# The low-part score products of the banded attention over all 128 rows, with zeros beside the keys' low parts

## The chip, the cores and the metric

One core of one Trainium2 chip runs the whole program. The metric is the device time of one execution in microseconds (us); the kernel before was run three times. A profile of one execution was taken beside the timed runs, and every row below is from it.

## What is computed

Two layers of a bidirectional encoder over 256 tokens with 1024 features. In each layer three branches are mixed (latent attention, a Fourier transform, banded attention), and a SwiGLU and a gated embedding follow. The change touches the scores of the banded attention alone:

```
q = q.reshape(B, nb, WIN_BLOCK, GQA_KV_HEADS, GQA_GROUP, GQA_HEAD_DIM)   # 2 key heads x 4 query heads, 64 wide
...
s = jnp.einsum('bnqhgd,bnkhd->bnhgqk', q, kw).astype(jnp.float32) * scale
s = s - slopes[None, None, :, :, None, None] * dist[:, :, None, None]
...
s = jnp.where(mask[None, :, None, None], s, -jnp.inf)
m = jnp.maximum(jnp.max(s, axis=-1, keepdims=True), sink_l)
e = jnp.exp(s - m)
probs = (e / (jnp.sum(e, axis=-1, keepdims=True) + jnp.exp(sink_l - m))).astype(v.dtype)
o = jnp.einsum('bnhgqk,bnkhd->bnqhgd', probs, vw)
```

There are 8 query heads of 64 features; heads 0 to 3 share the first key head ("left"), heads 4 to 7 the second ("right").

## The kernel before

**Numbers in two parts.** TensorE multiplies in a format that keeps 12 significant bits. Every float32 operand a is therefore split on chip into a high part H (a copy on ScalarE, rounded) and a low part L = a - H (a subtraction on VectorE), and a product takes three passes: H H, H L and L H. The weights stream in as chunks of eight 128 x 128 tiles (`w`, split to `wh` and `wl` at lines 175 and 180); activations live in the tiles `mixH` and `mixL` (in the code `A22` and `B22`: 22 slots of 128 x 256 each), `xs_...` (the layer's input) and others.

**Order of work.** A small planner in the program (class `Order`) writes the order of TensorE, ScalarE and VectorE out ahead of time, with assumed durations: 0.109 us for each product of 256 columns, whatever its rows. The main line is the products on TensorE; side chains (softmax, splits, norms) are woven in when the plan says that their data are there. On the chip each engine runs its own list in that order, and semaphores hold an instruction until its inputs are written. GpSimd (POOL) is not ordered by the planner: it does a few memsets, the norms' inverse roots (`rt_...`, line 497) and small copies.

**The banded attention.** In each layer `window_k` writes the keys and `window_qsplit` the queries. A head is 64 features wide, so a head's high and low parts fit on the 128 rows together: `qcs` holds, for a left head, the queries' high parts on rows 0 to 63 and their low parts on rows 64 to 127 (for a right head the other way round), and `kcs` holds the keys' high parts on both halves. One product of `qcs` with `kcs` over 128 rows is thus H H + L H. The third pass, the queries' H with the keys' L, takes only the 64 rows where the queries' high parts lie; the keys' low parts are in slot `KCI` of `B22`, the left head's on rows 0 to 63, the right head's on rows 64 to 127. `window_head` (8 per layer, two in flight, started 5.6 us apart in the plan) issues for each of two blocks of 128 queries the full product (line 977) and the 64-row product (line 978) into one tile `sc`; then VectorE adds the distances (line 289, out `sbc`), takes the maximum (line 984), ScalarE the exponentials, TensorE the transposes (`ptc`, line 924), and after a split (`phc`, `plc`) the products with the values (`po`, line 948). Between these steps TensorE does the Fourier transform (`pu`, `pab`, lines 317 to 319), the gates (`gp`) and the branches (`br`), lines 357, 358 and 364. Line 503 turns an inverse root into rows (`pr_...`), and cannot start before POOL's `rt_...`.

The latent attention later in the layer has heads of 128 rows: its scores (`sa`, lines 317 to 319 too) are three full passes for each block of queries.

Of the kernel before, what the change touches and what calls it, by code (L numbers as in the profile page):

```python
# [9 lines left out]
F32 = mybir.dt.float32  # L10
# [20 lines left out]
# the order of work is laid out with these times in us  # L31
T_MM = 0.109                # a float32r product with 256 columns
T_SEM = 0.18                # from one engine to another
MIX = "CCGGCCPPGPPGGBGGGBGGGBBG" # what fills attention's waits: Fourier channels and positions, gates, branches
TAB = 18.0                  # when the rotary tables are made
PACE = 5.6                  # from one head's start to the next
LATER = 0.3                 # how long a chain waits before its next step
ONACT = 2                   # of how many heads one is normed on ScalarE
STAGE = 3                   # buffers for weights as they come
WARM = (0.33, 0.15)         # how long TensorE is kept busy without data  # L40
URGENT = (4.5, 2.5)         # how far behind ScalarE and VectorE may be for splits to go on
LATE = (2, 2, 2)            # operand tiles left to a product's end
CT = 8                      # weight tiles of 128 x 128 per load
NCHUNK = 279

# columns of the constants' array
# [16 lines left out]
def dft_tiles():  # L63
    """The DFT over a group's 256 channels (cosines of 0..127, the alternating column, sines of
    1..127) and over the 256 positions, each with half of the orthonormal scale."""
    n = np.arange(256)
    cos = np.cos(2 * np.pi * (np.outer(n, n) % 256) / 256) / 16.0
    sin = np.sin(2 * np.pi * (np.outer(n, n) % 256) / 256) / 16.0
    m2 = np.concatenate([cos[:, :128], sin[:, :128]], axis=1)
    m2[:, 128] = cos[:, 128]  # L70
    return np.stack([m.reshape(2, P, SEQ).transpose(1, 0, 2) for m in (m2, cos, sin)]).astype(np.float32)
# [6 lines left out]
class Order:  # L78
    """Lays out the order of every engine's work: a main line of products on TensorE, and side chains
    that hand data from engine to engine. A chain gives the time at which its next piece's inputs  # L80
    should be there, and the piece goes in when the main line has come that far."""
# [19 lines left out]
    def run(self, engine, us, *deps):  # L101
        """an instruction on another engine; gives the time at which its result can be used"""
        at = max(self.free[engine], self.now, *deps)
        self.free[engine] = at + us
        return at + us + T_SEM

# [18 lines left out]
    def wait(self, at):  # L125
        """the main line needs something that is there at this time"""
        assert at < 1e8
        while self.now < at:
            to = min([at] + [max(t[0], self.now) for t in self.tasks])
            if self.warm:  # L130
                self.warm(to - self.now)
            self.now = to
            self.step()


class Weights:
    """The weights as one stream of 128 x 128 tiles in the order of their use; each is split on chip
    into two parts of 12 significant bits, w = H + L, both exact in float32r."""
# [17 lines left out]
    def pieces(self, c):  # L156
        n = CT * P // (1 if c else 2)       # the first chunk comes in halves
        return [slice(k, k + n) for k in range(0, CT * P, n)]

    def split(self):  # L160
        """a chain: the next chunk's parts, and the load of one more chunk"""
# [22 lines left out]
    def idle(self, engine, c, us):  # L184
        """waits while the engine has other work, unless the chunk is needed within this time"""
        O = self.O
        while (self.quiet or O.free[engine] > O.now + 0.1) and (c * CT - len(self.order)) * 3 * T_MM > us:
            yield O.now + 0.3

    def flush(self, n=0):  # L190
        """starts the splits that are due and have their buffers"""
        self.due += n
        while self.due and not self.using.get(len(self.parts) - 3):
            self.due -= 1
            self.O.start(self.split())

    def ready(self, n=1, high=False):
        """the time at which the next n tiles can be used"""
        c, at = (len(self.order) + n - 1) // CT, self.at_h if high else self.at
        return at[c] if c < len(at) else 1e9  # L200
# [21 lines left out]
def encoder(ctx: ExitStack, tc: tile.TileContext, order, gxT, pT, pos, cst, dftT, mask, sink, wts, outT):  # L222
# [21 lines left out]
    rd = {}                 # what chains have made, and when it can be used  # L244

# [16 lines left out]
    def drop(t, at=0.0):  # L262
        """its last use is in the order, and ends at this time"""
# [4 lines left out]
    def line(gen):  # L268
        """a chain's piece on the main line"""
# [31 lines left out]
    def need(key):  # L301
        """in a chain: goes on when this is there"""
# [5 lines left out]
    def have(key):  # L308
        """on the main line"""
# [24 lines left out]
    def mains(ps, keys, rhs, start=True, stop=True, skip=False, there=None):  # L334
        """a column tile's products over tiles of the contraction; those with a chunk's low parts come last"""
        i = 0
        while i < len(keys):
# [9 lines left out]
            # what the waits let in may have taken tiles  # L347
# [23 lines left out]
    def k_outer(pairs, key, rhs, done, late):  # L371
        """pairs of column tiles, each pair in a bank of its own, over the contraction's 8 tiles; over its
        last ones pair by pair"""
# [28 lines left out]
    def keep_warm(step):  # L402
        """while the main line waits, products of zeros hold TensorE's clock up"""
# [38 lines left out]
    class Squares:  # L442
        """sums of squares over feature tiles: six in pairs, and the last two one by one"""
# [4 lines left out]
        def add(self, src):  # L448
            """a chain's piece; src: [P, 2, SEQ]"""
# [21 lines left out]
        def total(self):  # L471
            """the pairs' sum"""
# [3 lines left out]
        def total1(self):  # L476
            """and the first single tile"""
# [12 lines left out]
    def rms_cols(ps, norms, name):  # L490
        """1/rms per token, as columns"""
# [8 lines left out]
    def rms_rows(pr, rt, n):  # L500
        """the columns as rows on every partition"""
# [4 lines left out]
    def rstd(parts, name):  # L506
        """parts: (tiles whose sum over partitions and tiles is the sum of squares, D, eps), up to two"""
# [29 lines left out]
    def pre_norm(st, name):  # L537
        """a chain: x's squares and the next products' 1/rms"""
# [11 lines left out]
    def post_norm(st, y, sq, i, nxt, name, want_squares, final=False, gname=None):  # L550
        """A chain: x += y * rstd(y) (times a gain if that isn't in y); splits the new x (times the next norm's gain) for
        the next products. Starts when seven tiles of y are under way."""
# [116 lines left out]
    def tables():  # L669
        """distances and rotary tables from the positions, where VectorE has time"""  # L670
# [63 lines left out]
    # columns and rows in the order that the chip takes them  # L734
# [16 lines left out]
    for i in range(DEPTH):  # L751
# [16 lines left out]
        g1 = [[cq[0], cq[1]], [cq[2], cq[3]], [kr, kc_cols], [vc_cols, qc_cols[0]]]  # L768
        z1 = [line(take("mm" if n < 3 else "s", f"z1{L}_{n}")) for n in range(4)]
        # the left heads' queries have their high parts in the upper rows and their low ones below, the right  # L770
        # heads' the other way round; the keys' high parts lie in both halves
        qcs = one.tile([P, 2, 4, SEQ], F32R, tag="qc", name=f"qc{L}")
        kcs = one.tile([P, 2, SEQ], F32R, tag="kc", name=f"kc{L}")
        up, low = slice(0, 64), slice(64, 128)

        def window_k(zk):
# [3 lines left out]
            for h, o, v in ((up, low, 0), (low, up, 1)):  # L780
                tt(256, B22[h, KCI, :], zk[h], kcs[h, v, :], ALU.subtract)
# [13 lines left out]
        # values: high and low columns of the left head, then low and high columns of the right head  # L795
# [101 lines left out]
        def probs_t(pb, src, neg, sums, h, name, extra=None):  # L897
            """softmax of src [P, 2, SEQ] over the keys; gives the transposed probabilities, split"""
# [37 lines left out]
        def pv_mm(key, off, side, v, ph, pl):  # L936
            """Values times probabilities. Two heads share an output tile: the left one's output has its main
            part (the values' high parts) in the upper rows and the rest in the lower ones, the right one's
            the other way round."""
# [28 lines left out]
        def window_head(j, side):  # L968
            h = j + 4 * side
            nm = f"c{L}_{h}"  # L970
            r = slice(64 * side, 64 * side + 64)
# [3 lines left out]
            for t in range(2):  # L975
                ts_ = slice(t * P, (t + 1) * P)
                T.matmul(sp[:, t, :], qcs[:, side, j, ts_], kcs[:, side, :], start=True, stop=False)
                T.matmul(sp[:, t, :], qcs[r, side, j, ts_], B22[r, KCI, :], start=False, stop=True)
# [276 lines left out]
        def normed(wname, kt, rhs, key, name, gname, *chain):  # L1255
# [13 lines left out]
            for n in range(3):  # L1269
                ps = line(take("mm", f"o{name}_{n}"))  # L1270
                late = kt - 2 if n == 0 else 0      # the first pair leaves the newest part of the operand to the end
# [116 lines left out]
def feature_major(a):  # L1388
    """[tokens, features] as [partition, feature tile, token]"""
# [66 lines left out]
```

## Time and profile before

| | us |
|---|---|
| median of three runs (lowest, highest) | 928.98 (927.42, 931.41) |
| span of the profiled execution | 928.1 |
| TensorE busy in it (matmuls) | 908.8, 98% |
| VectorE busy | 692.2, 75% |
| ScalarE busy | 547.6, 59% |
| POOL busy | 31.9, 3% |
| stretch with the banded attention, layer 0 | about 42.9 to 108 |
| the same, layer 1 | about 501.7 to 564 |

The span runs from the first to the last instruction of one execution and is all of its own time that the profile gives; it lies 0.9 below the median of the runs, inside what they cover. Busy time counts overlapping matmuls once; how fast TensorE goes is read from the distance between the starts of successive matmuls, not from their shown lengths, since a matmul of 0.28 us overlaps the next two.

### The profile page before, as it was taken

The page shows a single profiled execution, that of the slowest core. Times are in us where ns is not written, and L with a number is a line of the kernel's source. Part 1 is how long each engine was busy: PE and PEld are TensorE (multiplying, and loading weights), DVE is VectorE, ACT ScalarE, POOL GpSimd, SP SyncE. Part 2 cuts the span into 40 slices and gives each one's busy share as a digit, 9 for nine tenths or more (in the row PEclk, how much of TensorE's full clock was granted, in tenths as well). Part 3 has the DMA queues.
Part 4 walks back from the last instruction along what each step waited for, and adds up shares of the span by engine and source line. Part 5 has one row for each costly group of instructions (what it writes and reads, how often), then busy time and mean ns, then how long its engine had stood idle before and what let it go on. Part 6 is the DMA issues. An engine that isn't in the chain of part 4 may idle for free.

```text
span 928.1 us, 18352 instructions
## 1 busy us (share of the span) xinstructions
PE 908.8 (98%) x7497; PEld 894.3 (96%) x7497; DVE 692.2 (75%) x1066; ACT 547.6 (59%) x937; POOL 31.9 (3%) x46
## 2 busy tenths in 40 slices
PE   8999999999999999999999999999999999999995
PEld 7999999999999999999999999999999999999995
DVE  6888878886888777445789788887958977764575
ACT  6577776745655455444657776686465554444444
POOL 1200000000000000000002000000000000000001
PEclk9999999999999999999999999999999999999998
DMA  7631545455456655554554234445555566555552
GB/s 251 185 124 46 160 160 160 142 177 186 153 177 216 188 182 184 185 186 150 160 160 146 93 114 136 160 145 174 182 186 166 175 193 194 189 181 182 181 157 72
DMA packets 43845, 152.25 MB, mean 164 GB/s; under 512 B 5232, under 2 KB 6000, under 8 KB 43760
## 3 DMA queue, kind: packets, MB, share of 16 engines
q1 hardware_dynamic: 43760, 151.07, 51.3%
q8 instruction: 59, 0.97, 0.4%
q14 instruction: 26, 0.21, 0.1%
HBM read 150.00 MB, written 1.05 MB: 163 GB/s over the span
## 4 chain that ended last, share of the span: by engine, by line
PE 92%; issue 3%; DVE 2%; POOL 1%; DMA 1%; SPq 0%; ACT 0%; DVEq 0%; POOLq 0%
PE ffL L364 8%; PE ffL L357 8%; PE ffL L358 8%; PE gpL L364 5%; PE gpL L357 5%; PE ofL L364 5%; PE ofL L358 5%; PE ofL L357 5%; PE gpL L358 5%; PE ffL L385 4%; PE z1L L385 4%; PE brL L364 3%; PE brL L358 3%; PE brL L357 3%; PE omL L364 2%
## 5 line engine op out<-in xcount | busy, mean ns | idle before, releaser
L180 DVE TENSOR_TENSOR wl<-w,wh 128x1024 fp32r<-128x1024 f32 (+1 forms) x280 | 340.4, 1219 | 89.8 <-ACT wh L175 89.4
L175 ACT ACTIVATE wh<-w 128x1024 fp32r<-128x1024 f32 (+1 forms) x280 | 293.9, 1055 | 190.7 <-PE ofL L358 49.8
L357 PE MATMUL ffL<-xs_mixL,wh 128*128 128x256 f32 x608 | 146.9, 280 | 0.0
L358 PE MATMUL ffL<-xs_mixL,wh 128*128 128x256 f32 x608 | 146.7, 280 | 0.0
L358 PEld LDWEIGHTS ffL<-xs_mixL,wh 128*128 128x128 f32 x608 | 114.4, 188 | 0.0
L357 PEld LDWEIGHTS ffL<-xs_mixL,wh 128*128 128x128 f32 x608 | 114.2, 188 | 0.0
L358 PE MATMUL ofL<-hidL,wh 128*128 128x256 f32 x352 | 87.0, 283 | 0.0
L357 PE MATMUL ofL<-hidH,wh 128*128 128x256 f32 x352 | 86.9, 283 | 0.0
L364 PE MATMUL ffL<-xs_mixL,wl 128*128 128x256 f32 x608 | 85.8, 280 | 0.0
L364 PEld LDWEIGHTS ffL<-xs_mixL,wl 128*128 128x128 f32 x608 | 77.6, 188 | 0.0
L358 PEld LDWEIGHTS ofL<-hidL,wh 128*128 128x128 f32 x352 | 66.5, 189 | 0.0
L357 PEld LDWEIGHTS ofL<-hidH,wh 128*128 128x128 f32 x352 | 66.5, 189 | 0.0
L357 PE MATMUL brL<-mixH,wh 128*128 128x256 f32 x256 | 64.1, 283 | 0.0
L358 PE MATMUL brL<-mixL,wh 128*128 128x256 f32 x256 | 64.0, 283 | 0.0
L285 DVE TENSOR_TENSOR fzL<-ffL,R_pre_mixL 128x512 f32<-128x512 f32 x44 | 30.0, 690 | 31.1 <-PE ffL L364 31.0
L364 PE MATMUL ofL<-hidH,wl 128*128 128x256 f32 x352 | 52.2, 284 | 0.0
L358 PEld LDWEIGHTS brL<-mixL,wh 128*128 128x128 f32 x256 | 49.0, 191 | 0.0
L357 PEld LDWEIGHTS brL<-mixH,wh 128*128 128x128 f32 x256 | 49.0, 191 | 0.0
L357 PE MATMUL gpL<-xs_pleL,wh 128*128 128x256 f32 x192 | 48.5, 285 | 0.0
L357 PE MATMUL gpL<-xs_first,wh 128*128 128x256 f32 x192 | 48.1, 283 | 0.0
L358 PE MATMUL gpL<-xs_pleL,wh 128*128 128x256 f32 x192 | 47.6, 280 | 0.0
L358 PE MATMUL gpL<-xs_first,wh 128*128 128x256 f32 x192 | 47.4, 280 | 0.0
(424 smaller groups left out, 2041.3 us busy)
## 6 DMA issues: line engine op xcount, KB each, us to landing
w<-wts SPq DMA_DIRECT2D x278, 512.0 KB, 3.5
dftL<-dft SPq DMA_DIRECT2D x6, 256.0 KB, 3.4
gx<-gx SPq DMA_DIRECT2D x3, 256.0 KB, 6.8
outT<-gx SPq DMA_DIRECT2D x3, 256.0 KB, 2.3
w<-wts SPq DMA_DIRECT2D x2, 256.0 KB, 3.3
p<-pT SPq DMA_DIRECT2D x2, 256.0 KB, 3.7
dist<-mask SPq DMA_DIRECT2D x1, 256.0 KB, 5.5
outT<-gx SPq DMA_DIRECT2D x2, 128.0 KB, 2.4
```

The costliest lines, as they stand in the source:

```text
L175: self.nc.scalar.activation(h[:, s], w[:, s], AF.Copy)
L180: self.nc.vector.tensor_tensor(out=l[:, s], in0=w[:, s], in1=h[:, s], op=ALU.subtract)
L285: V.tensor_tensor(out=out, in0=a, in1=b, op=op)
L357: T.matmul(ps, w[j][0], rh, start=start and j == 0, stop=False, skip_group_check=skip)
L358: T.matmul(ps, w[j][0], rl, start=False, stop=False, skip_group_check=skip)
L364: T.matmul(ps, w[j][1], rhs(j)[0], start=False, stop=stop and j == len(keys) - 1, skip_group_check=skip)
L385: T.matmul(pairs[n][:, c, :], w[n][c][part], mov, start=(k == 0 and c == 0 and part == 0 and mov is xh), stop=False, skip_group_check=True)
```

## The change

The low-part product reads all 128 rows. For each key head there is now a slot of its own with its low parts on 64 rows and zeros on the other 64: the left head's in slot `KCI` of `A22` (which nothing used during this stage), the right head's where it was, in slot `KCI` of `B22`. Two memsets on GpSimd per layer write the zeros. The queries' tile is read whole, so the half with the queries' low parts meets the zeros. The diff also drops comments, which moves line numbers by three or four; nothing else differs. Its core:

```
+        kls = [A22[:, KCI, :], B22[:, KCI, :]]
+        for h, v in ((low, 0), (up, 1)):
+            G.memset(kls[v][h].bitcast(F32), 0.0)
+
         def window_k(zk):
             for h, o, v in ((up, low, 0), (low, up, 1)):
                 t = act(256, kcs[h, v, :], zk[h])
             yield t
             for h, o, v in ((up, low, 0), (low, up, 1)):
-                tt(256, B22[h, KCI, :], zk[h], kcs[h, v, :], ALU.subtract)
+                tt(256, kls[v][h], zk[h], kcs[h, v, :], ALU.subtract)
                 t = act(256, kcs[o, v, :], kcs[h, v, :])
...
         def window_head(j, side):
             h = j + 4 * side
             nm = f"c{L}_{h}"
-            r = slice(64 * side, 64 * side + 64)
...
             for t in range(2):
                 ts_ = slice(t * P, (t + 1) * P)
                 T.matmul(sp[:, t, :], qcs[:, side, j, ts_], kcs[:, side, :], start=True, stop=False)
-                T.matmul(sp[:, t, :], qcs[r, side, j, ts_], B22[r, KCI, :], start=False, stop=True)
+                T.matmul(sp[:, t, :], qcs[:, side, j, ts_], kls[side], start=False, stop=True)
                 O.spend(2 * T_MM)
```

TensorE's list around the first head of layer 0, before (`sc` is the head's scores, `kc` the keys' high parts, `qc` the queries; the size is that of the output):

```order
L364 MATMUL zq3L_567<-xs_first,wl_488 128x256 x2
L977 MATMUL scL_0_623<-kcL_141,qcL_140 128x256
L978 MATMUL scL_0_623<-mixL_135,qcL_140 128x256
L977 MATMUL scL_0_623<-kcL_141,qcL_140 128x256
L978 MATMUL scL_0_623<-mixL_135,qcL_140 128x256
L317 MATMUL puL_00_635<-mixH_134,xs_first 128x256
L318 MATMUL puL_00_635<-mixL_135,xs_first 128x256
L319 MATMUL puL_00_635<-mixH_134,xs_first 128x256
L503 MATMUL pr_latL_639<-cs,rt_latL_609 128x128 x4
```

and the same place in the changed kernel:

```order
L364 MATMUL zq3L_569<-xs_first,wl_490 128x256 x2
L980 MATMUL scL_0_625<-kcL_141,qcL_140 128x256
L981 MATMUL scL_0_625<-mixH_134,qcL_140 128x256
L980 MATMUL scL_0_625<-kcL_141,qcL_140 128x256
L981 MATMUL scL_0_625<-mixH_134,qcL_140 128x256
L317 MATMUL puL_00_637<-mixH_134,xs_first 128x256
L318 MATMUL puL_00_637<-mixL_135,xs_first 128x256
L319 MATMUL puL_00_637<-mixH_134,xs_first 128x256
L503 MATMUL pr_latL_641<-cs,rt_latL_611 128x128 x4
```

No product moved, was added or removed; a left head's second operand comes from `mixH` in place of `mixL`. The lists of ScalarE, VectorE and the DMA queue have the same instructions in the same order too.

POOL's list between the two layers, with the semaphores that each row waits for, before (`rt_ffL` is the inverse root of the norm after the SwiGLU of layer 0, `altL` a table of the next layer's Fourier step):

```order
L1105 MEMSET altL_6321 128x512 [waits DVE_49,PE_49]
L497 TENSOR_TENSOR rt_mixL_3166<-ms_mixL_3164,mhalf 128x2 [waits DVE_49]
L497 TENSOR_TENSOR rt_pre_mixL_3449<-ms_pre_mixL_3447,mhalf 128x2 [waits DVE_49]
L497 TENSOR_TENSOR rt_ffL_5476<-ms_ffL_5474,mhalf 128x2 [waits DVE_49,Pool_49]
L497 TENSOR_TENSOR rt_pleL_5829<-ms_pleL_5827,mhalf 128x2 [waits DVE_49]
```

and in the changed kernel:

```order
L1108 MEMSET altL_6325 128x512 [waits DVE_49,PE_49]
L497 TENSOR_TENSOR rt_mixL_3168<-ms_mixL_3166,mhalf 128x2 [waits DVE_49]
L497 TENSOR_TENSOR rt_pre_mixL_3451<-ms_pre_mixL_3449,mhalf 128x2 [waits DVE_49]
L778 MEMSET mixL_5862 64x256 [waits DVE_49,PE_49]
L778 MEMSET mixH_5861 64x256 [waits PE_49,Activation_49,Pool_49]
L497 TENSOR_TENSOR rt_ffL_5478<-ms_ffL_5476,mhalf 128x2 [waits DVE_49,Pool_49]
L497 TENSOR_TENSOR rt_pleL_5831<-ms_pleL_5829,mhalf 128x2 [waits DVE_49]
```

The memsets of layer 1 stand ahead of `rt_ffL` of layer 0. They write slots of the two big tiles, whose buffers the SwiGLU's hidden layer (`hidH`, `hidL`) holds until its last products (`of`, lines 358 and 364) have read it: that is their wait for PE. The memsets of layer 0 stand at the program's start, behind the memset of `mhalf`.

## Rows read from the trace of the kernel before

**Rows 1.** The page: busy time and share of the span, and its ending chain by engine.

```profile
PE 908.8 (98%) x7497; PEld 894.3 (96%) x7497; DVE 692.2 (75%) x1066; ACT 547.6 (59%) x937; POOL 31.9 (3%) x46
...
PE 92%; issue 3%; DVE 2%; POOL 1%; DMA 1%; SPq 0%; ACT 0%; DVEq 0%; POOLq 0%
```

**Rows 2.** Waits of PE, longest first: for whom; us in total, times, longest.

```profile
PE z1L L385 <- ACT wh L175: 2.9, 2, 2.0
PE ffL L385 <- DVE xs_mixL L289: 1.6, 2, 0.8
PE pr_pleL L503 <- POOL rt_pleL L497: 1.4, 2, 1.2
PE warm L414 <- POOL zeros L399: 1.1, 1, 1.1
PE pgL L385 <- DVE xs_ffL L285: 1.0, 2, 0.5
PE pr_latL L503 <- POOL rt_latL L497: 1.0, 1, 1.0
```

**Rows 3.** The tile of the scores: durations min/median/max ns, first and last start.

```profile
L977 PE MATMUL scL<-kcL,qcL x32: 278/332/388, 42.9 to 563.0; 128*128 128x256 f32 x32
L978 PEld LDWEIGHTS scL<-mixL,qcL x32: 182/183/183, 43.1 to 563.3; 64*128 64x128 f32 x32
L978 PE MATMUL scL<-mixL,qcL x32: 378/381/384, 43.1 to 563.3; 64*128 64x256 f32 x32
...
  DVE sbcL L289: 15.1, 11
```

**Rows 4.** Timeline of PE around layer 0's second head: start us, length us.

```profile
51.25 0.28 PE L358 MATMUL gpL<-xs_first,wh 128*128 128x256 f32 x1
51.37 0.28 PE L977 MATMUL scL<-kcL,qcL 128*128 128x256 f32 x1
51.58 0.38 PE L978 MATMUL scL<-mixL,qcL 64*128 64x256 f32 x1
51.89 0.39 PE L977 MATMUL scL<-kcL,qcL 128*128 128x256 f32 x1
52.20 0.38 PE L978 MATMUL scL<-mixL,qcL 64*128 64x256 f32 x1
52.51 0.39 PE L357 MATMUL gpL<-xs_first,wh 128*128 128x256 f32 x1
52.74 0.28 PE L358 MATMUL gpL<-xs_first,wh 128*128 128x256 f32 x1
```

**Rows 5.** Timeline of PE at a latent-attention head's scores, and their weight loads (tile view).

```profile
127.10 0.28 PE L318 MATMUL saL0h<-kpL,mqL 128*128 128x256 f32 x1
127.22 0.28 PE L319 MATMUL saL0h<-kpL,mqL 128*128 128x256 f32 x1
127.34 0.28 PE L317 MATMUL saL0h<-kpL,mqL 128*128 128x256 f32 x1
127.46 0.28 PE L318 MATMUL saL0h<-kpL,mqL 128*128 128x256 f32 x1
127.58 0.28 PE L319 MATMUL saL0h<-kpL,mqL 128*128 128x256 f32 x1
127.70 0.28 PE L357 MATMUL gpL<-xs_first,wh 128*128 128x256 f32 x1
...
L318 PEld LDWEIGHTS saL0h<-kpL,mqL x16: 187/189/192, 127.0 to 181.2; 128*128 128x128 f32 x16
```

**Rows 6.** Timeline of PE: a head followed by transposes, and transposes alone.

```profile
72.95 0.28 PE L977 MATMUL scL<-kcL,qcL 128*128 128x256 f32 x1
...
74.09 0.65 PE L924 MATMUL ptcL<-cs,sbcL 128*128 128x128 f32 x4
74.51 0.37 PE L357 MATMUL gpL<-xs_first,wh 128*128 128x256 f32 x1
...
60.80 0.60 PE L924 MATMUL ptcL<-cs,sbcL 128*128 128x128 f32 x4
61.15 0.36 PE L357 MATMUL gpL<-xs_first,wh 128*128 128x256 f32 x1
```

**Rows 7.** Timelines of PE, PEld and POOL at layer 0's first head.

```profile
42.91 0.28 PE L977 MATMUL scL<-kcL,qcL 128*128 128x256 f32 x1
...
44.65 1.61 PE L503 MATMUL pr_latL<-cs,rt_latL 128*128 128x128 f32 x7
...
44.64 1.53 PEld L503 LDWEIGHTS pr_latL<-cs,rt_latL 128*128 128x128 f32 x8 [0.17 <-POOL rt_latL L497]
...
43.07 1.52 POOL L497 TENSOR_TENSOR rt_latL<-ms_latL,mhalf 128x4 f32<-128x4 f32 x1 [5.73 <-DVE ms_latL L293]
```

**Rows 8.** Timeline of ScalarE: the first head's probabilities, scaled before their transposes.

```profile
59.23 0.90 ACT L281 ACTIVATE sbcL<-sbcL,invcL 128x256 f32<-128x256 f32 x2
```

**Rows 9.** Stretches: busy us of each engine (count), PE's granted clock, DMA.

```profile
44.00:46.00 2.00, 2.00 (x11) 1.77 (x11) 1.94 (x3) 0.00 (x0) 0.59 (x1) 0.74 0.16 18
46.00:48.00 2.00, 2.00 (x12) 2.00 (x11) 1.93 (x4) 0.60 (x1) 0.00 (x0) 0.50 0.74 254
48.00:50.00 2.00, 2.00 (x17) 2.00 (x17) 1.96 (x7) 1.46 (x4) 0.30 (x1) 0.91 0.48 133
```

**Rows 10.** Timelines of POOL at the start, and of PE and POOL at layer 0's end.

```profile
0.98 0.20 POOL L422 MEMSET ones<- 128x128 f32 x1
...
1.62 0.52 POOL L1105 MEMSET altL<- 128x512 f32 x1
...
430.84 1.12 PE L364 MATMUL ofL<-hidH,wl 128*128 128x256 f32 x8
...
433.39 0.70 POOL L497 TENSOR_TENSOR rt_ffL<-ms_ffL,mhalf 128x2 f32<-128x2 f32 x1 [169.70 <-DVE ms_ffL L293]
```

More of the change, by code (lines that the diff above doesn't have):

```diff
@@ L774, in encoder @@
         up, low = slice(0, 64), slice(64, 128)
+        kls = [A22[:, KCI, :], B22[:, KCI, :]]
+        for h, v in ((low, 0), (up, 1)):
+            G.memset(kls[v][h].bitcast(F32), 0.0)
         def window_k(zk):
@@ L780, in window_k @@
             for h, o, v in ((up, low, 0), (low, up, 1)):
-                tt(256, B22[h, KCI, :], zk[h], kcs[h, v, :], ALU.subtract)
+                tt(256, kls[v][h], zk[h], kcs[h, v, :], ALU.subtract)
                 t = act(256, kcs[o, v, :], kcs[h, v, :])
@@ L970, in window_head @@
             nm = f"c{L}_{h}"
-            r = slice(64 * side, 64 * side + 64)
             for k in (("kc",), ("q", j), "dist", ("vc",)):
@@ L977, in window_head @@
                 T.matmul(sp[:, t, :], qcs[:, side, j, ts_], kcs[:, side, :], start=True, stop=False)
-                T.matmul(sp[:, t, :], qcs[r, side, j, ts_], B22[r, KCI, :], start=False, stop=True)
+                T.matmul(sp[:, t, :], qcs[:, side, j, ts_], kls[side], start=False, stop=True)
                 O.spend(2 * T_MM)
```

## Prediction

> **What bounds the kernel now.** I read the page first: TensorE is busy for 908.8 of 928.1 us, and the chain that ended last is 92% PE [rows 1]. Busy time of overlapping matmuls does not prove a bound, so next the waits of PE: the six longest kinds come to 9.0 us of 928, in the prologue, at the norms, and once in front of `pr_lat` [rows 2]; none stands at a score, a transpose or a product with the values. TensorE's own list sets the time in both stretches with the banded attention. What is to be looked for is how far apart TensorE's matmuls start.
>
> For that, the tile of the scores and the timeline. A product of 256 columns over 128 rows starts 0.12 us after the one before: the scores of a latent-attention head go 127.10, 127.22, 127.34, 127.46, 127.58, 127.70 [rows 5]. Around a banded head the steps are 0.21, 0.31, 0.31, 0.31 and then, already between two full products of the gates, 0.23 [rows 4]. None of it is a wait for data: PE has none there [rows 2], and the 64-row products look the same at all 16 heads, 378 to 384 ns each of 32 [rows 3]. The steps are long wherever the 64-row product is, on either side of it; with 128 rows on both sides they are short.
>
> **The change part by part.** *The products.* Their number and order stay; 32 of 64 become full [rows 3]. If each then starts 0.12 after the last, a head followed by ordinary products gives: from 51.37 to 52.74 there are five steps, 1.37 us; five steps of 0.12 are 0.60; gain 0.77 [rows 4, 5]. In three of the 16 heads transposes follow: from 72.95 to 74.51 it is 1.56 us; four steps of 0.12 and the 0.35 that four transposes take elsewhere (60.80 to 61.15) are 0.83; gain 0.73 [rows 6].
>
> *Where the gain is lost at once.* In the first head of layer 0 three Fourier products follow, and then `pr_lat`, which waits for POOL's `rt_lat`: POOL starts it at 43.07 and needs 1.52 us, to 44.59, and `pr_lat` starts at 44.65 [rows 7]. Nothing of the change makes `rt_lat` earlier, so TensorE arrives sooner and waits: this head gives nothing. The sum is 12 x 0.77 + 3 x 0.73 = 11.4 us.
>
> *What is late next.* Every engine behind TensorE gets its scores sooner: VectorE now idles for them 15.1 us in 11 heads [rows 3]. But TensorE also comes sooner to what a chain must deliver. The tightest place that I found is the first head's transposes at 60.80: ScalarE scales the probabilities from 59.23 to 60.13, 0.67 earlier [rows 6, 8], and one shortened head (0.77) lies between; ScalarE's own work there gains less. So a few tenths may be lost there, and perhaps once more in the Fourier steps. Bounds: nothing, or in the worst case the 0.77 of one head at two or three places, 2 us. I take 0.4, nearer to the lower end, since PE waits nowhere in these stretches today but for `pr_lat` [rows 2].
>
> *The clock.* The granted clock falls to half for 3.4 us in 44 to 50 of layer 0 (0.74, 0.50, 0.91 of three stretches of 2 us: 0.52 + 1.00 + 0.18 = 1.70 us lost) [rows 9], behind a run of tiny matmuls, the slow scores and the wait for `rt_lat`. The same work, with more waiting, will lie ahead of it, so I leave it as it is; if it does not fall there any more, 1.7 us more are gained, and one more fall elsewhere costs as much.
>
> *The zeros.* Two memsets of 64 x 256 for each layer. The trace has none of this size; 128 x 128 took 0.20 us and 128 x 512 0.52 [rows 10]. These are the bounds; by the columns 0.31 is near, so 0.6 for the pair. In layer 0 they run at about 1.2 us, with nothing due on POOL but memsets. In layer 1 they stand ahead of `rt_ffL`, on which the norm and all that follows hangs. They wait for the last product that reads the hidden layer, which ends at 430.84 + 1.12 = 431.96; they are through at about 432.6 to 433.1, and `rt_ffL` could not start before 433.39 for its own data [rows 10]. The norm's wait covers them, with 0.3 to 0.8 to spare; without that cover they would cost 0.6. The low parts' subtractions on VectorE keep their size and number: nothing.
>
> *Sum.* 928.1 - 11.4 + 0.4 = 917.1 for the profiled execution; its span lies 0.9 below the median of the runs (928.98), so the time should be 918.0.
>
> **The rivals.**
> *Half of it is lost in the softmax chains.* TensorE would wait at the transposes and at the products with the values, because VectorE and ScalarE cannot go faster. If each of the 15 heads loses 0.4 of its 0.77, that is 6 us: 923.6. For it speaks the 0.67 of slack at 60.80 [rows 6, 8]; against it that VectorE itself is kept waiting for scores [rows 3], and that PE has no wait in this stretch today [rows 2].
>
> *It isn't the 64 rows.* The long steps could come from the operands (queries as weights, two products into one half of a bank) or another property that stays. Then nothing changes: 929. Against it: the latent attention's scores are the same pattern, queries as weights into a score tile, with no long step [rows 5]. For it: the first step, 0.21, differs from the three others, so more than one cause is at work; if the 0.09 of that step stayed in each head, only 1.4 us of the gain would go.
>
> *Weight loads no longer overlap: slower.* A full product's weight load (0.19 us) would have to stand between its product and the one before, instead of running beside it. With 0.19 + 0.28 = 0.47 for each step, five steps take 2.35 us in place of 1.37, and 16 heads cost 15.7 us: 944. It decides from 0.27 us a step upward (1.37 / 5). Against it: in the latent attention the loads are just as long, 0.189, and the steps are 0.12, so they do overlap [rows 5]. The Trainium skill, page "TensorE: Matmul & The Clock Gate", section "Part 3: Packing small matmuls — row/col tiling", says that a weight load overlaps with running matmuls only when their row groups differ, and advises to put products of few rows on row groups of their own, where they run concurrently. By that rule this change goes the wrong way, towards the 944 above; the trace does not agree, since loads and products over the same 128 rows overlap in it, at 0.12 a step against 0.31 with 64 rows.
>
> **How the numbers follow.** The forecast, 918.0, has 0.77 of the chance; half of it lost, 0.12; no effect, 0.07; slower, 0.04. The forecast's own range is 915 to 920: all 16 heads (0.8 more) and no fall of the clock (1.7 more) below, the first step's 1.4 and some stalls above. With the runs' own scatter (927.42 to 931.41) and towards the half-lost case I give 914.8 to 922.0. What a measurement of this kernel can tell from no change is about 0.5%, 4.6 us, so faster means under 924.3: the first case and nearly all of the second, 0.88; the same 0.08; slower 0.04.
>
> **What the profile of the changed kernel would show.** Right: steps of 0.12 through every `sc` product and the one behind it, the low-part products at 0.28 in place of 0.38 us; a wait of PE or its weight loads in front of `pr_lat` in layer 0, longer by 0.4 to 0.8 than the 0.17 now [rows 7]; two memsets on POOL between 432.0 and 433.1, less what came earlier, and `rt_ffL` right behind its data; the stretch up to the last head some 4.5 us shorter in layer 0 and 6 in layer 1, and the rest of the span unchanged. Wrong: steps that stay at 0.31 (no effect), of 0.3 to 0.5 (the loads), or new waits of PE at `ptc`, `po` or `pab` of more than a few tenths each (the chains).

## The result and the profile after

The changed kernel takes 919.5 us (918.68 to 919.92), the kernel before 929.79 beside it (927.42 to 931.41): a ratio of 0.989, with a 95% interval of 0.9863 to 0.9917. The forecast was 918.0, the range 914.8 to 922.0. The profiled execution has a span of 917.2 us (forecast 917.1) and took 919.09. That the two spans agree to 0.1 us is partly luck, as the section on the prediction shows.

The page of the changed kernel, in the columns of [rows 1], engine, busy us, share, instructions:

```profile
PE 897.5 (98%) x7497; PEld 890.2 (97%) x7497; DVE 690.5 (75%) x1066; ACT 546.9 (60%) x937; POOL 34.5 (4%) x50
```

TensorE has the same 7497 matmuls, POOL four instructions more (the memsets). What changed is how far apart the matmuls start. First the tile of the scores, as in [rows 3] (durations min/median/max ns), with the line on VectorE's idle time for them:

```profile
L980 PE MATMUL scL<-kcL,qcL x32: 277/282/287, 42.0 to 551.1; 128*128 128x256 f32 x32
L981 PE MATMUL scL<-mixH,qcL x16: 278/283/286, 42.1 to 545.1; 128*128 128x256 f32 x16
L981 PE MATMUL scL<-mixL,qcL x16: 278/282/287, 49.0 to 551.2; 128*128 128x256 f32 x16
...
  DVE sbcL L289: 6.3, 9
```

All 64 products now last 277 to 287 ns. Before, the products on 64 rows took 378 to 384, and the full ones beside them up to 388. VectorE idles 6.3 us for scores in place of 15.1. Then the timeline of PE at the second head of layer 0, the place of [rows 4]:

```profile
48.86 0.28 PE L980 MATMUL scL<-kcL,qcL 128*128 128x256 f32 x1
48.98 0.28 PE L981 MATMUL scL<-mixL,qcL 128*128 128x256 f32 x1
49.10 0.28 PE L980 MATMUL scL<-kcL,qcL 128*128 128x256 f32 x1
49.22 0.28 PE L981 MATMUL scL<-mixL,qcL 128*128 128x256 f32 x1
49.33 0.28 PE L357 MATMUL gpL<-xs_first,wh 128*128 128x256 f32 x1
49.45 0.28 PE L358 MATMUL gpL<-xs_first,wh 128*128 128x256 f32 x1
```

The five steps from the first score to the second product of the gates are 0.12, 0.12, 0.12, 0.11 and 0.12, in sum 0.59 us; in [rows 4] they are 0.21, 0.31, 0.31, 0.31 and 0.23, in sum 1.37. Where a head's scores meet the wait for `rt_lat`, at the first head (timelines of PE, PEld and POOL, as in [rows 7]; in square brackets is the idle time before, and who ended it):

```profile
42.44 0.28 PE L317 MATMUL puL<-mixH,xs_first 128*128 128x256 f32 x1
42.83 0.39 PE L318 MATMUL puL<-mixL,xs_first 128*128 128x256 f32 x1
...
43.70 1.16 PE L503 MATMUL pr_latL<-cs,rt_latL 128*128 128x128 f32 x8 [0.38 <-POOL rt_latL L497]
...
42.83 0.19 PEld L318 LDWEIGHTS puL<-mixL,xs_first 128*128 128x128 f32 x1 [0.31 <-DVE mixL L285]
...
43.70 0.97 PEld L503 LDWEIGHTS pr_latL<-cs,rt_latL 128*128 128x128 f32 x8 [0.58 <-POOL rt_latL L497]
...
42.13 1.52 POOL L497 TENSOR_TENSOR rt_latL<-ms_latL,mhalf 128x4 f32<-128x4 f32 x1 [5.69 <-DVE ms_latL L293]
```

POOL is through at 42.13 + 1.52 = 43.65, and `pr_lat` starts 0.05 later; before it was 0.06 behind 44.59. What the four scores save there comes back as two waits, one at the Fourier product of line 318 for VectorE, one of the weight loads at `pr_lat` (0.58, before 0.17).

The clearest measure of the change is not the span but the stretch from a layer's first score to the gates' first product behind its last head. The profile of before has the fall of the clock of [rows 9] inside it, so both kernels were profiled once more, and neither had the fall. The ends of the two stretches in the second profile of the kernel before:

```profile
41.25 0.28 PE L977 MATMUL scL<-kcL,qcL 128*128 128x256 f32 x1
...
104.86 0.28 PE L357 MATMUL gpL<-xs_first,wh 128*128 128x256 f32 x1
...
498.49 0.28 PE L977 MATMUL scL<-kcL,qcL 128*128 128x256 f32 x1
...
560.73 0.29 PE L357 MATMUL gpL<-xs_pleL,wh 128*128 128x256 f32 x1
```

and in the second profile of the changed kernel:

```profile
41.49 0.28 PE L980 MATMUL scL<-kcL,qcL 128*128 128x256 f32 x1
...
100.11 0.28 PE L357 MATMUL gpL<-xs_first,wh 128*128 128x256 f32 x1
...
493.55 0.28 PE L980 MATMUL scL<-kcL,qcL 128*128 128x256 f32 x1
...
549.73 0.28 PE L357 MATMUL gpL<-xs_pleL,wh 128*128 128x256 f32 x1
```

Layer 0 goes from 63.61 to 58.62 us, layer 1 from 62.24 to 56.18: 11.05 us together. The forecast for this was 11.4 - 0.4 = 11.0. The stretches repeat well (58.60 and 56.17 in the first profile after), while the spans of one kernel's runs lie up to 4.7 us apart (926.8 to 931.5 in the ten of the kernel with the zeros alone).

### The profile page after: what moved, and what is told of

Same layout as the page of the kernel before. It is cut to its first block, busy times and chain, and to the rows that moved or that the text cites. A ratio compares the mean times of both kernels' runs of the same rounds, so it can differ in the third digit from the quotient of the medians.

```text
span 917.2 us, 18357 instructions
## 1 busy us (share of the span) xinstructions
PE 897.5 (98%) x7497; PEld 890.2 (97%) x7497; DVE 690.5 (75%) x1066; ACT 546.9 (60%) x937; POOL 34.5 (4%) x50
## 4 chain that ended last, share of the span: by engine, by line
PE 90%; issue 4%; DVE 2%; POOL 2%; DMA 1%; ACT 0%; SPq 0%; DVEq 0%; POOLq 0%; ACTq 0%
PE ffL L364 8%; PE ffL L358 8%; PE ffL L357 8%; PE gpL L364 5%; PE ofL L364 5%; PE ofL L358 5%; PE ofL L357 5%; PE gpL L358 5%; PE gpL L357 5%; PE ffL L385 4%; PE brL L364 3%; PE brL L358 3%; PE brL L357 3%; PE z1L L385 2%; PE omL L364 2%
## 5 line engine op out<-in xcount | busy, mean ns | idle before, releaser
L357 PE MATMUL ffL<-xs_mixL,wh 128*128 128x256 f32 x608 | 148.4, 281 | 0.0
L358 PE MATMUL ffL<-xs_mixL,wh 128*128 128x256 f32 x608 | 148.2, 281 | 0.0
```

The lines of the kernel that those rows point to most:

```text
L357: T.matmul(ps, w[j][0], rh, start=start and j == 0, stop=False, skip_group_check=skip)
L358: T.matmul(ps, w[j][0], rl, start=False, stop=False, skip_group_check=skip)
```

## The experiments

The theory was that the time goes where the number of rows changes from one product to the next, at each change; the rivals, that each product on 64 rows costs by itself, or that the long steps have little to do with the rows. In the table the stretch is the one just defined, with layer 0 and layer 1; the times under "before" are those of the kernel before, timed beside it.

| kernel | time, us | before, us | ratio (95%) | stretch, us | sum |
|---|---|---|---|---|---|
| before, second profile | 929.29 (one run) | 927.58 | | 63.61 + 62.24 | 125.85 |
| changed, first profile | 919.5 | 929.79 | 0.989 (0.9863 to 0.9917) | 58.60 + 56.17 | 114.77 |
| changed, second profile | 917.79 | 927.58 | 0.9892 (0.9875 to 0.9908) | 58.62 + 56.18 | 114.80 |
| zeros made, 64 rows used | 930.49 | 930.04 | 1.0007 (0.9993 to 1.002) | 63.62 + 62.27 | 125.89 |
| left heads alone full | 924.69 | 930.04 | 0.9938 (0.9923 to 0.9953) | 61.65 + 59.19 | 120.84 |
| 64 rows, like beside like | 922.98 | 930.04 | 0.9926 (0.9904 to 0.9948) | 61.14 + 59.06 | 120.20 |
| one of two low products full | 925.54 (one run) | 930.35 (one run) | | 61.09 + 59.12 | 120.21 |
| first head on 64 rows | 918.16 (one run) | 927.58 | | 58.63 + 56.14 | 114.77 |

**The zeros without their use.** The memsets stay, and the products go back to 64 rows:

```diff
-                T.matmul(sp[:, t, :], qcs[:, side, j, ts_], kls[side], start=False, stop=True)
+                r = low if side else up
+                T.matmul(sp[:, t, :], qcs[r, side, j, ts_], kls[side][r], start=False, stop=True)
```

> The two memsets of each layer and the left heads' new slot, with the low-part products still on 64 rows. My theory (the number of rows of the low-part product is what costs): no change, ratio 0.995 to 1.005, and the steps around a head stay 0.21, 0.31, 0.31, 0.31, 0.23 us. Rival (the gain comes from where the left heads' low parts lie, or from the memsets' effect on POOL's order): a ratio near that of the change, 0.989, or steps of 0.12 in the left heads. Rival (the zeros cost something that the gain hid): ratio above 1.003.

The ratio is 1.0007 and the stretch 125.89 against 125.85: nothing is gained by the new layout, and the four memsets cost nothing that the runs can tell. The whole gain hangs on the rows of the products.

**The left heads alone.**

```diff
-        for h, v in ((low, 0), (up, 1)):
+        for h, v in ((low, 0),):
...
-                T.matmul(sp[:, t, :], qcs[:, side, j, ts_], kls[side], start=False, stop=True)
+                r = slice(0, P) if side == 0 else low
+                T.matmul(sp[:, t, :], qcs[r, side, j, ts_], kls[side][r], start=False, stop=True)
```

> Only the left heads (8 of 16) take the low-part product over 128 rows; the right heads keep 64 rows and need no zeros. My theory (each head gains on its own, the first head of layer 0 nothing): 5 x 0.77 + 2 x 0.73 = 5.3 us of the 11.4, ratio near 0.994; steps of 0.12 in left heads and of 0.21 to 0.31 in right ones. Rival (TensorE is then held by the softmax chains, so that the first heads shortened give most): more than 7 us. Rival (the 0.77 per head is only had when both heads in flight are short): under 3 us.

Timeline of PE: a right head, still on 64 rows, and then a left one.

```profile
49.69 0.28 PE L980 MATMUL scL<-kcL,qcL 128*128 128x256 f32 x1
49.90 0.38 PE L982 MATMUL scL<-mixL,qcL 64*128 64x256 f32 x1
50.21 0.39 PE L980 MATMUL scL<-kcL,qcL 128*128 128x256 f32 x1
...
64.27 0.28 PE L980 MATMUL scL<-kcL,qcL 128*128 128x256 f32 x1
64.39 0.28 PE L982 MATMUL scL<-mixH,qcL 128*128 128x256 f32 x1
64.51 0.28 PE L980 MATMUL scL<-kcL,qcL 128*128 128x256 f32 x1
```

Steps of 0.21 and 0.31 at the right head, 0.12 at the left one. The stretches are 5.0 us shorter, near the theory's 5.3 and far from both rivals. Layer 1 gives 3.05, where three heads at 0.77 and one before transposes at 0.72 make 3.03. Layer 0 gives 1.96, where the first head gives nothing and the other three make 2.28; 0.19 of the difference goes back at one Fourier product (`pab`). The gain comes head by head.

**64 rows, like beside like.** All products of the kernel before, with both full products of a head first and then both on 64 rows, so that the rows change twice in a head and not four times. The mark `start`, which opens a sum, now stands on the tile's first product alone:

```diff
+            r = low if side else up
             for t in range(2):
                 ts_ = slice(t * P, (t + 1) * P)
-                T.matmul(sp[:, t, :], qcs[:, side, j, ts_], kcs[:, side, :], start=True, stop=False)
-                T.matmul(sp[:, t, :], qcs[:, side, j, ts_], kls[side], start=False, stop=True)
+                T.matmul(sp[:, t, :], qcs[:, side, j, ts_], kcs[:, side, :], start=(t == 0), stop=False, skip_group_check=True)
+            for t in range(2):
+                ts_ = slice(t * P, (t + 1) * P)
+                T.matmul(sp[:, t, :], qcs[r, side, j, ts_], kls[side][r], start=False, stop=True, skip_group_check=True)
```

> The low-part products stay on 64 rows, but each head issues both full products first and then both 64-row products, so that the number of rows changes twice per head in place of four times. Theory A (what costs is the change between 128 and 64 rows on TensorE): steps of 0.12 (full to full), 0.21, 0.12 (64 to 64), 0.31, 0.23, so 0.99 us for five steps in place of 1.37 and a gain of 0.38 for each of 15 heads, 5.7 us, ratio near 0.994. Theory B (each 64-row product has a long step of its own, whatever stands beside it): 0.12, 0.21, 0.31, 0.31, 0.23, a gain of 0.19 per head, 2.9 us, ratio near 0.997.

Timeline of PE at the second head (two of a kind stand in one row, x2), and last that of its weight loads:

```profile
49.17 0.40 PE L981 MATMUL scL<-kcL,qcL 128*128 128x256 f32 x2
49.50 0.50 PE L984 MATMUL scL<-mixL,qcL 64*128 64x256 f32 x2
49.93 0.39 PE L357 MATMUL gpL<-xs_first,wh 128*128 128x256 f32 x1
50.16 0.28 PE L358 MATMUL gpL<-xs_first,wh 128*128 128x256 f32 x1
```

The second products of the two pairs by themselves:

```profile
49.29 0.28 PE L981 MATMUL scL<-kcL,qcL 128*128 128x256 f32 x1
...
49.72 0.28 PE L984 MATMUL scL<-mixL,qcL 64*128 64x256 f32 x1
```

```profile
49.06 0.30 PEld L981 LDWEIGHTS scL<-kcL,qcL 128*128 128x128 f32 x2
49.50 0.29 PEld L984 LDWEIGHTS scL<-mixL,qcL 64*128 64x128 f32 x2
49.93 0.19 PEld L357 LDWEIGHTS gpL<-xs_first,wh 128*128 128x128 f32 x1
```

Half of the gain is there with not one product on 64 rows fewer: the stretch is 120.20, 5.65 less than before, where the changed kernel has 11.05. Theory A had 5.7, theory B 2.9. From the first score to the gates' second product it is 50.16 - 49.17 = 0.99 us, between 1.37 and 0.59, as theory A had it. Its single steps were not right: it had 0.12, 0.21, 0.12, 0.31, 0.23, and the starts give 0.12, 0.21, 0.22, 0.21, 0.23. The loads show where a change costs. A full product's load runs ahead of it (49.06 for 49.17). Where the rows change, load and product start together (49.50 and 49.50, 49.93 and 49.93), and the product after that comes late once more (0.22 to 49.72, 0.23 to 50.16). So each change adds about 0.09 on the step to it and 0.10 on the step behind, 0.19 in all; where changes follow one another both fall on one step, 0.12 + 0.19 = 0.31, which is the middle step of [rows 4]. The second 64-row product is shown 0.28 us long, like a full one; the 0.38 of [rows 3] goes with the change before it. What holds the load back at a change is not shown.

**One of the two low products full.** The number of changes is again two, but only one product of a head stays on 64 rows:

```diff
-                T.matmul(sp[:, t, :], qcs[:, side, j, ts_], kls[side], start=False, stop=True)
+                r = (low if side else up) if t else slice(0, P)
+                T.matmul(sp[:, t, :], qcs[r, side, j, ts_], kls[side][r], start=False, stop=True)
```

> The changed kernel with only the second block's low-part product of each head back on 64 rows: one 64-row product per head, so two changes of the number of rows, as many changes as with both 64-row products side by side, and half of the products. Theory A (each change of the number of rows costs 0.19 us, whatever the count of products): 0.12, 0.12, 0.21, 0.31, 0.22 us, 0.38 us per head more than the changed kernel, so first score to last about 5.7 us longer than there. Theory C (each 64-row product costs 0.19 us and so do the two changes only once, which fits the grouped kernel as well): about 0.19 us per head, 2.9 us.

Timeline of PE at the second head:

```profile
49.31 0.28 PE L980 MATMUL scL<-kcL,qcL 128*128 128x256 f32 x1
49.43 0.28 PE L982 MATMUL scL<-mixL,qcL 128*128 128x256 f32 x1
49.55 0.28 PE L980 MATMUL scL<-kcL,qcL 128*128 128x256 f32 x1
49.76 0.38 PE L982 MATMUL scL<-mixL,qcL 64*128 64x256 f32 x1
50.07 0.38 PE L357 MATMUL gpL<-xs_first,wh 128*128 128x256 f32 x1
50.29 0.28 PE L358 MATMUL gpL<-xs_first,wh 128*128 128x256 f32 x1
```

The sum of the stretches is 120.21, that of the kernel with two such products in a head 120.20. That is 5.4 us above the changed kernel, where theory A had 5.7 and theory C 2.9, and the steps are theory A's. One product on 64 rows costs as much as two side by side: the price belongs to the change of the number of rows, not to the product. Order and `start` marks are here those of the changed kernel, so the other marks of the grouped one are not what cost there. The whole time, 925.54, lies above the grouped kernel's 922.98, and most of that comes from outside the heads: in this profile the first products of the SwiGLU go at 118.7 ns in both layers, in the grouped one's at 117.3, some 2.4 us (last section).

**The first head on 64 rows.**

```diff
-                T.matmul(sp[:, t, :], qcs[:, side, j, ts_], kls[side], start=False, stop=True)
+                r = up if i == 0 and h == 0 else slice(0, P)
+                T.matmul(sp[:, t, :], qcs[r, side, j, ts_], kls[side][r], start=False, stop=True)
```

> The changed kernel with the low-part products of the first head of layer 0 back on 64 rows, all else as changed. My theory (behind this head TensorE waits for the inverse root on GpSimd, so that its gain is lost at once): the product behind that wait starts within 0.1 us of the inverse root's end in both, so the span is the changed kernel's, within what two executions differ by. Rival (the gain of this head counts): 0.77 us more, all of it in front of that product, which then starts more than 0.3 us after the inverse root's end.

Timelines of POOL and PE at `pr_lat` of layer 0:

```profile
42.89 1.52 POOL L497 TENSOR_TENSOR rt_latL<-ms_latL,mhalf 128x4 f32<-128x4 f32 x1 [5.70 <-DVE ms_latL L293]
```

```profile
44.10 0.28 PE L318 MATMUL puL<-mixL,xs_first 128*128 128x256 f32 x1
44.22 0.28 PE L319 MATMUL puL<-mixH,xs_first 128*128 128x256 f32 x1
44.47 0.38 PE L503 MATMUL pr_latL<-cs,rt_latL 128*128 128x128 f32 x1
```

The long steps are back (0.21, 0.31, 0.31, 0.31) and `pr_lat` still follows 0.06 behind the end of `rt_lat` (44.41). Layer 0's stretch is 58.63 against 58.60 and 58.62: this head's scores are free in either form.

**Both kernels once more.** No edit; for the spread of single profiles and for the clock.

> The kernel before once more, for a second profile. Two things differ between the profiles of before and after outside the heads: the granted clock fell to half for 3.4 us behind the first head of layer 0 before and not after, and the products of the SwiGLU's first part start 117.3 ns apart before and 118.7 after. If these belong to the kernel, this profile shows the fall near 45 us and 117.3 ns again; if they belong to the single execution, one or both come out otherwise.

> The changed kernel once more. Ratio to the kernel before 0.988 to 0.991 (11.0 us of 930, less what differs from run to run). If the missing fall of the clock behind the first head and the 118.7 ns of the SwiGLU belong to the kernel, this profile shows both again; if to the single execution, one or both come out otherwise.

These are the profiles that gave the 11.05 us. Neither shows the fall of the clock in 44 to 50. The SwiGLU's steps came out otherwise too: 117.3 ns in layer 0 and 120.0 in layer 1 of the kernel before, 117.3 in both layers of the changed one. So both belong to the single execution.

## Why the prediction was right, step by step

*A head gives 0.77, or 0.73 before transposes.* Right. Start by start, the heads gain 0.77 to 0.79, and those followed by transposes 0.72 to 0.73. The reason was right in kind, but the prediction stopped at "the steps are long wherever the 64-row product is"; the experiments sharpen it to 0.19 us for each change. It also answers the rival's point that the first step, 0.21, differs from the others: no second cause is needed, since the first step holds one part of one change and a middle step the parts of two.

*The first head of layer 0 gives nothing.* Right, shown by the kernel that leaves it on 64 rows. One reading beside it was off: the wait of 1.0 us at `pr_lat` in [rows 2] is layer 1's and ends at 498.24, before that layer's first score. In layer 0 only the weight load waited, the 0.17 of [rows 7].

*0.4 is lost in chains.* Right: the 15 heads gain 11.45 us together in the second profiles and the stretches 11.05, so 0.40 is given back. Most of it, 0.17 and 0.19, goes at the two places in layer 0 that the prediction named, the first head's transposes (`ptc`, a wait for ScalarE) and a Fourier product (`pab`). The stretch of layer 0 is 5.0 us shorter, where the prediction had 4.5, that of layer 1 the 6 that it had. The waits of PEld in the changed kernel have both, in total us, times and longest:

```profile
PEld ptcL L928 <- ACT sbcL L281: 0.2, 1, 0.2
PEld pabL L317 <- issue: 0.2, 1, 0.2
```

So the softmax chains kept up, and the rival in which half the gain is lost falls.

*The zeros are hidden.* Right, with the margin a little better than 0.3 to 0.8. The timeline of POOL at the end of layer 0, to be held against [rows 10]:

```profile
424.77 0.30 POOL L778 MEMSET mixL<- 64x256 f32 x1 [168.57 <-PE ofL L358]
425.81 0.31 POOL L778 MEMSET mixH<- 64x256 f32 x1 [0.74 <-PE ofL L364]
427.09 0.70 POOL L497 TENSOR_TENSOR rt_ffL<-ms_ffL,mhalf 128x2 f32<-128x2 f32 x1 [0.97 <-DVE ms_ffL L293]
```

The memsets take 0.30 and 0.31, as estimated; one goes already before the hidden layer's last products end. POOL then idles 0.97 us for the norm's own data.

*The clock stays as it was.* Wrong for the profile after. The middle one of the three stretches of [rows 9], where the granted clock was 0.50, in the changed kernel and then in the second profile of the kernel before (PEclk is the third number from the end):

```profile
46.00:48.00 2.00, 2.00 (x19) 2.00 (x18) 1.93 (x5) 1.92 (x4) 0.19 (x1) 1.00 0.86 290
```

```profile
46.00:48.00 2.00, 2.00 (x19) 2.00 (x18) 1.96 (x6) 1.95 (x6) 0.19 (x1) 1.00 0.53 150
```

The granted clock is 1.00 there and in the stretches beside it, with the change and without it, and with the zeros alone too. The fall belonged to one execution and not to the kernel, and taking it as fixed was the wrong reading.

*The weight loads.* The rival that would have made the kernel slower falls: over 128 rows after 128 rows the loads run ahead and the steps stay at 0.12. The Trainium skill, page "TensorE: Matmul & The Clock Gate", section "Part 3: Packing small matmuls — row/col tiling", lists loads as overlapping with running matmuls only across different row groups, though the same section also lets a load run ahead that goes to the background weight buffer. The trace does not agree with the first: of the two loads that fill 49.06 to 49.36 above, the second runs beside the product of 49.17, over the same 128 rows. The Trainium skill, page "TensorEngine Tiling (Array Packing)", section "Key Properties", says that "Changing tiling mode (not just tile) drains the TensorE". The trace fits this, at 0.19 us for a change from 128 to 64 rows or back, if products on 64 and on 128 rows count as two modes; a drain itself is not in the trace, and the page gives no size.

*The step that was mis-sized: 0.9 from the span to the time.* The prediction took the difference of the profiled span (928.1) and the median of other executions (928.98). In every run whose own span and time are known, the time lies 1.7 to 2.0 above the span (919.09 and 917.2; 929.29 and 927.5; 916.12 and 914.3). With 1.85 the forecast would have been 918.95, against 919.5.

*Luck in the span.* From the first profile of before (928.1) to that of after (917.2) it is 10.9. The parts: 11.05 of the change and 1.55 of the clock's fall (127.4 against 125.85 for the stretches); the first score stands at 41.97 in place of 42.91, 0.94 less; and in the SwiGLU's first products about 2.4 us more (below). 11.05 + 1.55 + 0.94 - 2.4 = 11.1, near the 10.9. Terms of 1 to 2 us that have nothing to do with the change nearly cancelled.

## What to carry to other kernels

Read how far apart matmuls start, not how long they are said to last: at this kernel PE was 98% busy and had no wait at the scores, while 64 products there lost 11 us in their steps. Keep the number of rows the same along a run of matmuls; a product on half the rows among full ones pays at each change, here 0.19 us, so fill it with zeros where these are cheap, or at least put the halves side by side, which here gave half of the gain with no product reading a zero. To price an edit of 1%, compare a stretch between two named instructions in several profiles; single spans carry clock falls and other scatter of the same size.

## What the runs showed that was not expected

The first products of the SwiGLU, a plain run without waits, go at slightly different speeds from execution to execution, at full granted clock. Stretches of 50 us with the instructions of the tile `ff` alone (behind PE's busy time the number of its matmuls; PEclk and DMA at the end): the first profile of before in layer 0, its second one in layer 1, and the changed kernel in layer 0.

```profile
290.00:340.00 50.00, 50.00 (x429) 50.00 (x428) 5.59 (x9) 1.00 0.60 190
```

```profile
740.00:790.00 50.00, 50.00 (x419) 50.00 (x418) 6.23 (x9) 1.00 0.57 189
```

```profile
290.00:340.00 50.00, 50.00 (x424) 50.00 (x423) 6.22 (x9) 1.00 0.60 186
```

About 429, 424 or 419 matmuls fit. From start to start a layer's products show a mean step of 117.3, 118.7 or 120.0 ns and nothing between: in the nine profiles each of the two layers fell on one of the three, and the kernel before and the changed one each had more than one of them. For some 912 products a layer, one level is about 1.2 us. That is why the profile of after lost some 2.4 us there: it has 118.7 in both layers, the first profile of before 117.3. The cause stays open; nothing here was tried on it. Also open is whether the price of a change is the same between other numbers of rows than 128 and 64, and whether going from the upper to the lower 64 rows costs anything.
